# A state-space and attention trunk in one kernel: loads, low parts and stages of the state space parameters reordered

## The chip, the core and the metric

The kernel runs on one core of a Trainium2 chip: TensorE (PE; its weight loads are PEld), VectorE (DVE), ScalarE (ACT), GpSimd (POOL) and SyncE (SP, which only issues DMAs here). The metric is the device time in microseconds of one execution; lower is better. Each engine works its instructions off in program order; DMAs are issued from the queues of SP, ACT and POOL.

## What is computed

Two layers over x of 512 tokens by 2048 features, float32. Layer 0 mixes with a diagonal complex state space (S5), layer 1 with sparse attention over shared keys and values; each ends in a layer norm of the residual. The change touches the start of layer 0 only:

```python
def s5_mixer(x, w_in, lam_re, lam_im, log_dt, b_re, b_im, c_re, c_im, d_skip, w_glu, b_glu, w_out):
    u, z = jnp.split(x @ w_in, 2, axis=-1)          # 2048 -> 1024 + 1024
    dt = jnp.exp(log_dt)[:, None]                   # 64 groups
    mag = jnp.exp(lr * dt)
    ar, ai = mag * jnp.cos(li * dt), mag * jnp.sin(li * dt)     # 64 groups x 64 states
    ...                                             # b scaled by a function of ar, ai, lr, li
    h = scan(a, b u)                                # over the 512 tokens
    y = real(c h) + d_skip * u
    g = gelu(y)
    y = g * sigmoid(g @ w_glu + b_glu)
    return (y * silu(z)) @ w_out
```

## The kernel before

**Products in three parts.** TensorE multiplies in a reduced float32 form. Each operand is split into a high part (a cast on ScalarE) and a low part (value minus high part), and `mm3` issues three matmuls: high by high (L235), high by low (L236), low by high (L237). `Weights` streams weights in units of 128 x 1024: a load on SP's queue into one of 3 buffers, the cast on ScalarE (L78), the low part on VectorE (L85). From unit 11 (`DMA_FROM`) up to the gate weights the low part is made otherwise: ScalarE writes minus the high part (L81), and a DMA from GpSimd's queue adds the weights to it (L82). There are 3 buffers of split weights.

**The loop of layer 0** (`layer0_in`). x arrives in 16 slabs of 128 x 512 over 7 buffers. For each slab k: the load of slab k + 3, the cast (L788), the low part (L789: on VectorE for k in `XL_DVE`, on GpSimd for k = 2 to 9), and, on every second k, the split of the weight unit after the current one; then four `mm3`, one for each of the output tiles u0 to u3 that accumulate over all slabs. Units 0 to 8 serve this loop. Then come twelve tiles (`L0_TILES`: u4, z0, u5, z1, ...) of 16 `mm3` each, two units a tile: units 9 and 10 for u4, 11 and 12 for z0, 13 and 14 for u5. Unit j is split two `mm3` into the unit two before it.

**Work between the products.** `Background` holds four lanes of generators. After each `mm3` a tick adds 3 to a counter and advances one lane that is due (two lanes in the tiles), the one due longest first; a generator's yielded number is the gap until it is due again. So the counter fixes where an instruction stands in each engine's queue: 12 a slab, 192 for the loop, 48 a tile, 768 for all tiles. Nothing moves an instruction at run time.

**Lane 0 is the state space chain** (`S5.chain`). First the parameters (`params`), steps with a gap of `PACE`: the loads; three steps of exponential of the step size; four of sine and cosine of the angle, the last of which sets up the rotations on lane 2; three of exponential of the magnitude; then products, three doublings of powers and two small steps. All of it is VectorE work on 128x64 values. Then the letters of `START`, one every 3 counts: t is a step of the tables of group 0 (11 steps: six of VectorE work, two of TensorE products, a subtraction, a store, and the loads and transposes), p one of the tables of group 1, r one of the rotation of group 0, b waits for the end of the loop, a dot is an empty step. Then, for each of 8 groups of channels, the 18 tokens of `CYCLE` (54 counts): a is the scan of this group, t and p tables of the next two, r the next rotation.

**Lane 2** runs `turns` on GpSimd: 16 steps (`TPACE` 8) of repeated angle doublings (L465 to L479), products that fill two tables RB and RA (L484 to L489) and sign changes (L500, L502). A rotation (r) on VectorE reads these tables and waits for them in the program order.

**The queue of GpSimd before:** the zero fill of a DRAM buffer's padding (L342, L343), four loads of the two halves of lambda, the load of the step size broadcast over 128 rows (L369), then low parts of x, raw loads for tables (L350, L352), rotation steps and the DMAs of L82, in the order of the counter.

Of the kernel before, what the change touches and what calls it, by code (L numbers as in the profile page):

```python
# [11 lines left out]
F32 = mybir.dt.float32  # L12
# [3 lines left out]
OP = mybir.AluOpType  # L16
# [21 lines left out]
class Weights:  # L38
# [4 lines left out]
    def __init__(self, nc, pool, units):  # L43
        self.nc, self.pool, self.units = nc, pool, units
        self.extra, self.side, self.whole = {}, {}, set()
        self.pool_units = set()
        self.by_dma = set()
        self.raw, self.hl = {}, {}
        self.nd = self.ns = 0
# [261 lines left out]
def paced(gen, gap):  # L311
    for _ in gen:
        yield gap


PAD = 16 * (L - 1)


class S5:
# [6 lines left out]
    def __init__(self, c, sc, gT, bg):  # L326
        tc = c.tc
        self.bg, self.U = bg, {}
        self.u_d = c.dram.tile([8, GP, 16, L, NCH], F32, name="u_d")
        self.y_d = c.dram.tile([8, L, 16, GP, NCH], F32, name="ys_d")  # L330
        self.c, self.tc, self.nc, self.A, self.ident, self.gT = c, tc, tc.nc, c.A, c.ident, gT
        self.p1 = sc.enter_context(tc.tile_pool(name="s5p", reuse_waits="tile", bufs=1, side="right"))
        self.tb = sc.enter_context(tc.tile_pool(name="s5t", reuse_waits="tile", bufs=1, side="right"))
        self.ps = sc.enter_context(tc.tile_pool(name="s5ps", reuse_waits="tile", bufs=1, space=PSUM, side="right"))
        self.tab, self.raw, self.rot = {}, {}, {}
        self.summed = self.done = -1
        self.turned = False
        self.banks = False

        self.k_d = c.dram.tile([8, GP, 16, PAD + 128], F32, name="k_d")  # L340
        zero = self.tb.tile([64, PAD], F32, tag="ta", name="zero")
        self.nc.gpsimd.memset(zero, 0.0)  # L342
        self.nc.gpsimd.dma_start(self.k_d[:, :, :, :PAD].rearrange("t g c n -> (t g) c n"),  # L343
                                 zero.unsqueeze(1).to_broadcast([64, 16, PAD]))

    def load(self, ct):
        if ct >= 8 or ct in self.raw:
# [7 lines left out]
    def params(self):  # L355
        nc, A, p1 = self.nc, self.A, self.p1
        V, S, P, SP = nc.vector, nc.scalar, nc.gpsimd, nc.sync
        scratch = self.tb.tile([128, 18, G], F32, tag="W1", name="scratch", bufs=2)
        pw = self.tb.tile([128, 17 * G], F32, tag="tb", name="pw")
        slot = iter(range(18))  # L360

        def new(nm):
            return scratch[:, next(slot)]

        lr, li, ld = new("lr"), new("li"), new("ld")
        for h in range(2):
            P.dma_start(lr[64 * h:64 * h + 64], A["lam_re"])
            P.dma_start(li[64 * h:64 * h + 64], A["lam_im"])
        P.dma_start(ld, A["log_dt"].partition_broadcast(128))  # L369
        sg = p1.tile([128, 1], F32, name="sg")  # L370
        V.memset(sg[0:64], 1.0)
        V.memset(sg[64:128], -1.0)
        self.sg = sg
        dt, x, mag, th = new("dt"), new("x"), new("mag"), new("th")
        a, b, c, d = new("ta"), new("tb"), new("tc"), new("td")
        e = new("te")
        ni = new("ni").bitcast(I32)
        yield
        yield from exp_f32(V, ld, a, b, c, ni, dt)
        V.tensor_tensor(x, lr, dt, OP.mult)  # L380
        V.tensor_tensor(th, li, dt, OP.mult)
        sn, cs = new("sn"), new("cs")
        yield from sincos_f32(V, th, a, b, c, d, e, sn, cs)
        self.load(0)
        self.bg.add(2, self.turns(cs, sn, e, ld, dt, new("tf"), th, new("tg"), new("th2")))
        yield from exp_f32(V, x, a, b, c, ni, mag)
        yield
        X = pw[:, 512:].rearrange("p (g n) -> p g n", n=9)
        Y = p1.tile([128, G, 9], F32, name="Y")
        Xs = p1.tile([128, G, 9], F32, name="Xs")  # L390
        V.memset(X[:, :, 0:1], 1.0)
        V.memset(Y[:, :, 0:1], 0.0)
        ar, ai = X[:, :, 1], Y[:, :, 1]
        V.tensor_tensor(ar, mag, cs, OP.mult)
        V.tensor_tensor(ai, mag, sn, OP.mult)
        yield
        V.tensor_tensor(a, lr, lr, OP.mult)
        V.tensor_tensor(b, li, li, OP.mult)
        V.tensor_tensor(a, a, b, OP.add)
        inv = x  # L400
        V.reciprocal(inv, a)
        am1 = d
        V.tensor_scalar(am1, ar, -1.0, None, OP.add)
        cr = p1.tile([128, G], F32, name="cr")
        sci = p1.tile([128, G], F32, name="sci")
        V.tensor_tensor(a, am1, lr, OP.mult)
        V.tensor_tensor(b, ai, li, OP.mult)
        V.tensor_tensor(a, a, b, OP.add)
        V.tensor_tensor(cr, a, inv, OP.mult)
        V.tensor_tensor(a, ai, lr, OP.mult)  # L410
        V.tensor_tensor(b, am1, li, OP.mult)
        V.tensor_tensor(a, a, b, OP.subtract)
        V.tensor_tensor(a, a, inv, OP.mult)
        V.tensor_scalar(sci, a, sg, -1.0, OP.mult, OP.mult)
        self.cr, self.sci = cr, sci
        yield

        for lo, n in ((1, 1), (1, 2), (1, 4)):
            m = lo + n - 1
            shp = [128, G, n]  # L420
            xa, ya = X[:, :, lo:lo + n], Y[:, :, lo:lo + n]
            xm, ym = X[:, :, m:m + 1], Y[:, :, m:m + 1]
            if n > 1:
                xm, ym = xm.to_broadcast(shp), ym.to_broadcast(shp)
            t1 = pw[:, 0:256].rearrange("p (g n) -> p g n", n=4)[:, :, :n]
            t2 = pw[:, 256:512].rearrange("p (g n) -> p g n", n=4)[:, :, :n]
            dst = slice(m + 1, m + 1 + n)
            V.tensor_tensor(t1, xa, xm, OP.mult)
            V.tensor_tensor(t2, ya, ym, OP.mult)
            V.tensor_tensor(X[:, :, dst], t1, t2, OP.subtract)  # L430
            V.tensor_tensor(t1, xa, ym, OP.mult)
            V.tensor_tensor(t2, ya, xm, OP.mult)
            V.tensor_tensor(Y[:, :, dst], t1, t2, OP.add)
            yield
        V.tensor_scalar(Xs, X, sg, None, OP.mult)
        self.Y, self.Xs = Y, Xs
        yield

        m8 = p1.tile([128, G], F32, name="m8")
        V.tensor_tensor(m8, mag, mag, OP.mult)  # L440
        V.tensor_tensor(m8, m8, m8, OP.mult)
        V.tensor_tensor(m8, m8, m8, OP.mult)
        self.m8 = m8
        yield
# [236 lines left out]
    def chain(self):  # L681

        yield from paced(self.params(), PACE)
        t, p, r = self.tables(0), self.tables(1), self.rotation(0)
        for what in START:
            if what == "r":
# [20 lines left out]

XL_DVE = (0, 1, 10, 11, 12, 13, 14, 15)  # L710

TPACE = 8
PACE = 9

DMA_FROM = 11
EARLY = 2
# [2 lines left out]
SLOT = 3  # L719


START = 'ttttttb....ttttt.rprppp'
CYCLE = 'a a t a t a tt t rt ar a t a p a p ap p'

L0_TILES = [('u', 4), ('z', 0), ('u', 5), ('z', 1), ('u', 6), ('z', 2), ('z', 3), ('u', 7), ('z', 4), ('z', 5), ('z', 6), ('z', 7)]
# [2 lines left out]
def layer0_in(c, sc, sz_d):  # L728

    tc, nc, A, W, index, mm3, split = c.tc, c.nc, c.A, c.W, c.index, c.mm3, c.split  # L730
    V, S, P, PE, SP = nc.vector, nc.scalar, nc.gpsimd, nc.tensor, nc.sync
    xh = c.xp.tile([128, KD, T], F32R, tag="xh", name="xh")
    xl = c.xp.tile([128, KD, T], F32R, tag="xl", name="xl")
# [6 lines left out]
    bg = Background(4)  # L740
# [33 lines left out]
            SP.dma_start(xr[k], A["xT"][k])  # L774

    bg.add(0, s5.chain())
    pss = [pj.tile([128, T], F32, tag="ps", name="ps") for _ in range(2)]
    pss += [s5.ps.tile([128, T], F32, tag="tp", name="ps", bufs=2) for _ in range(2)]
    load_x(0)
# [3 lines left out]
    for u, ks in enumerate([(0,), (1,)] + [(k, k + 1) for k in range(2, KD, 2)]):  # L783
        h, l = W.get(u, 0, 1)
        for k in ks:
            load_x(k + 3)
            x = xr.pop(k)
            S.copy(xh[:, k], x)  # L788
            (V if k in XL_DVE else P).tensor_tensor(xl[:, k], x, xh[:, k].bitcast(F32), OP.subtract)  # L789
            if k == ks[-1]:  # L790
                W.ahead(u + 1)
            for n in range(4):
                lo = 512 * (k - ks[0]) + 128 * n
                ns = slice(lo, lo + 128)
                mm3(pss[n], h[:, ns], l[:, ns], xh[:, k], xl[:, k], k == 0, k == KD - 1)
                bg.tick()
# [9 lines left out]
    for what in L0_TILES:  # L806
# [4 lines left out]
        for u in range(2):  # L811
            h, l = W.get(index[what] + u, 1)
# [7 lines left out]
        n = what[1]  # L820
# [15 lines left out]
    for k in range(KE):  # L836
# [4 lines left out]
        for n in range(2):  # L841
            h, l = hls[n]
# [24 lines left out]
    for n in range(KE):  # L867
# [3 lines left out]
        else:  # L871
            h, l = W.get(index["w_glu", n])
# [4 lines left out]
        z = zs.pop(n)  # L877
# [766 lines left out]
```

## Time and profile before

| | |
|---|---|
| median of 3 runs (lowest, highest) | 1816.9 us (1815.18, 1820.62) |
| profiled execution | 1814.74 us, its span 1813.0 us |
| granted TensorE clock, mean over the span | 0.986 |
| busy, share of the span | PE 97%, PEld 80%, DVE 55%, ACT 33%, POOL 10% |
| HBM traffic | 188.42 MB read, 19.86 MB written, 115 GB/s |

The span runs from the first to the last instruction; the execution's time lies 1.7 us above it. Busy shares are means over stages that differ: the loop of layer 0 fills some 70 us, its tiles reach to 294 us, layer 1 takes the rest. A wait in brackets names the instruction whose end released the waiting one, as far as the semaphores show it.

### The profile page before, as it was taken

To read this page: it belongs to the slowest core of one execution; us is meant where nothing else is said; L and a number is where in the kernel's file an instruction comes from. 1 tells how busy PE (TensorE), PEld (TensorE's weight loads), DVE (VectorE), ACT (ScalarE), POOL (GpSimd) and SP (SyncE) were. 2 spreads that over 40 slices of the span, in tenths; PEclk is the share of its full clock that TensorE was granted. 3 is DMA by queue.
4 is the path that set the end of the run, shared out by engine and by line. 5 is a ranking of instruction groups with operands and counts; after the bars stand their busy time and mean duration, and the time that the engine had idled before them with its cause. 6 is when DMAs were issued, how large, how long until landed. Compare 5 with 4: busy or idle time off the path is not lost.

```text
span 1813.0 us, 21852 instructions
## 1 busy us (share of the span) xinstructions
PE 1753.1 (97%) x8455; PEld 1455.5 (80%) x8455; DVE 1005.7 (55%) x1807; ACT 605.3 (33%) x1018; POOL 187.7 (10%) x241
## 2 busy tenths in 40 slices
PE   6889999998999999999999999999999999999997
PEld 5668877886888888888888888888888888888886
DVE  7778863549333366553555553555543555665346
ACT  3344443323333333332333332333332333333120
POOL 5921100006100000000000000000000000010000
PEclk8999999999999999999999999999999999999999
DMA  5468774543333322222222222222222322236343
GB/s 202 147 151 213 199 178 127 197 151 135 128 102 119 105 82 87 76 87 82 87 70 87 87 76 93 87 77 81 88 87 82 99 76 82 76 115 233 127 140 104
DMA packets 89751, 209.70 MB, mean 116 GB/s; under 512 B 25264, under 2 KB 34720, under 8 KB 88624
## 3 DMA queue, kind: packets, MB, share of 16 engines
q1 hardware_dynamic: 81008, 181.31, 30.4%
q0 software_dynamic: 6336, 22.81, 5.3%
q10 hardware_dynamic: 2304, 4.20, 0.6%
q8 instruction: 66, 1.08, 0.2%
q14 instruction: 37, 0.30, 0.1%
HBM read 188.42 MB, written 19.86 MB: 115 GB/s over the span
## 4 chain that ended last, share of the span: by engine, by line
PE 81%; DVE 3%; ACT 1%; issue 0%; DVEq 0%; ACTq 0%
PE ps L235 23%; PE ps L237 23%; PE ps L236 23%; PE tp L1448 2%; PE s L237 1%; PE s L235 1%; PE s L236 1%; PE o L236 1%; PE o L237 1%; PE o L235 1%; DVE v L959 1%; PE cps L1213 1%; PE tp L1413 0%; PE tp L999 0%; PE o L1422 0%
## 5 line engine op out<-in xcount | busy, mean ns | idle before, releaser
L235 PE MATMUL ps<-x1h,hl 128*128 128x512 f32 (+1 forms) x1440 | 564.8, 392 | 1.6 <-ACT hl L78 1.6
L237 PE MATMUL ps<-x1h,hl 128*128 128x512 f32 (+1 forms) x1440 | 557.8, 387 | 0.5 <-DVE hl L85 0.5
L236 PE MATMUL ps<-x1l,hl 128*128 128x512 f32 (+1 forms) x1440 | 556.8, 387 | 0.0
L85 DVE TENSOR_TENSOR hl<-wr,hl 128x1024 fp32r<-128x1024 f32 (+1 forms) x247 | 300.6, 1221 | 321.0 <-ACT hl L78 317.4
L78 ACT CAST hl<-wr 128x1024 fp32r<-128x1024 f32 (+1 forms) x273 | 284.4, 1045 | 219.3 <-PE ps L237 185.5
L237 PEld LDWEIGHTS ps<-x1h,hl 128*128 128x128 f32 x1440 | 271.6, 189 | 57.1 <-DVE hl L85 1.0
L235 PEld LDWEIGHTS ps<-x1h,hl 128*128 128x128 f32 x1440 | 272.0, 189 | 48.2 <-ACT hl L78 1.8
L236 PEld LDWEIGHTS ps<-x1l,hl 128*128 128x128 f32 x1440 | 272.0, 189 | 46.2
L1385 ACT ACTIVATE p<-s,m 128x384 f32<-128x384 f32 (+3 forms) x128 | 67.6, 528 | 358.3 <-DVE m L1384 355.8
L1321 POOL TENSOR_TENSOR y<-y,z 128x512 f32<-128x512 f32 x32 | 41.5, 1296 | 999.8 <-DVE z L1320 863.0
L241 DVE TENSOR_TENSOR pl<-tp,ph 128x512 fp32r<-128x512 f32 (+3 forms) x128 | 61.9, 488 | 109.3 <-ACT ph L240 109.0
L236 PE MATMUL ps<-xl,hl 128*128 128x512 f32 x256 | 104.8, 409 | 11.9 <-DVE xl L789 6.9
L235 PE MATMUL ps<-xh,hl 128*128 128x512 f32 x256 | 110.3, 431 | 6.1 <-ACT xh L788 6.1
L237 PE MATMUL ps<-xh,hl 128*128 128x512 f32 x256 | 104.6, 409 | 6.2 <-DMA hl<-w_in_b 6.2
L240 ACT CAST ph<-tp 128x512 fp32r<-128x512 f32 (+3 forms) x128 | 54.1, 426 | 150.6 <-PE tp L1448 150.3
L235 PE MATMUL ps<-hl,y1h 128*128 128x512 f32 x256 | 99.7, 389 | 0.0
L236 PE MATMUL ps<-hl,y1h 128*128 128x512 f32 x256 | 99.6, 389 | 0.0
L237 PE MATMUL ps<-hl,y1l 128*128 128x512 f32 x256 | 99.6, 389 | 0.0
L236 PEld LDWEIGHTS ps<-xl,hl 128*128 128x128 f32 x256 | 50.8, 198 | 23.1 <-DVE xl L789 8.8
L1384 DVE TENSOR_REDUCE m<-s 128x1 f32<-128x384 f32 (+3 forms) x128 | 62.9, 491 | 4.4
L237 PEld LDWEIGHTS ps<-xh,hl 128*128 128x128 f32 x256 | 50.5, 197 | 18.4 <-DMA hl<-w_in_b 7.1
L1307 DVE SCALAR_TENSOR_TENSOR z<-z,ps 128x512 f32<-128x512 f32 x48 | 33.0, 688 | 57.5 <-ACT z L1306 57.4
(351 smaller groups left out, 2328.8 us busy)
## 6 DMA issues: line engine op xcount, KB each, us to landing
wr<-b_w_in SPq DMA_DIRECT2D x128, 512.0 KB, 3.2
wr<-kv_w SPq DMA_DIRECT2D x48, 512.0 KB, 3.2
wr<-b_w_out SPq DMA_DIRECT2D x32, 512.0 KB, 3.3
wr<-w_in_b SPq DMA_DIRECT2D x24, 512.0 KB, 3.7
hl<-w_in_b POOLq DMA_DIRECT2D x22, 512.0 KB, 6.4
wr<-w_out SPq DMA_DIRECT2D x16, 512.0 KB, 3.6
xr<-xT SPq DMA_DIRECT2D x16, 256.0 KB, 3.8
Tz<-k_d SPq DMA_DIRECT2D x64, 64.0 KB, 2.4
```

Of the source, the lines that this page charges most:

```text
L78: self.nc.scalar.copy(h[:, :n], r[:, :n])
L85: eng.tensor_tensor(l[:, :n], r[:, :n], h[:, :n].bitcast(F32), OP.subtract)
L235: PE.matmul(o, sh, mh, start=start, stop=False)
L236: PE.matmul(o, sh, ml, start=False, stop=False)
L237: PE.matmul(o, sl, mh, start=False, stop=stop)
L240: self.nc.scalar.copy(h, src)
L241: self.nc.vector.tensor_tensor(l, src, h.bitcast(F32), OP.subtract)
L1307: self.nc.vector.scalar_tensor_tensor(z, z, 1.0, ps, OP.add, OP.mult)
L1321: P.tensor_tensor(y[0], y[0], z, OP.add)
L1384: self.nc.vector.tensor_reduce(m[:, b - 1, i:i + 1], s, AX.X, OP.max, negate=True)
L1385: self.nc.scalar.activation(self.p[h, b][i], s, AF.Exp, bias=m[:, b - 1, i:i + 1], accum_out=self.sums[h, b][:, i:i + 1])
L1448: PE.transpose(tp[:, 128 * (i - j):128 * (i - j) + 128], p[i][:, at:at + 128], ident)
```

## The change

Four things. The step size is loaded first, ahead of lambda, and the zero fill comes behind these loads; the chain is advanced once before the loop instead of at the loop's first tick. All 16 low parts of x are made by VectorE. `PACE` goes from 9 to 12. `START` puts group 0's tables and three steps of group 1's tables ahead of the two rotation steps.

```diff
@@ -338,10 +338,6 @@
         self.banks = False
 
         self.k_d = c.dram.tile([8, GP, 16, PAD + 128], F32, name="k_d")
-        zero = self.tb.tile([64, PAD], F32, tag="ta", name="zero")
-        self.nc.gpsimd.memset(zero, 0.0)
-        self.nc.gpsimd.dma_start(self.k_d[:, :, :, :PAD].rearrange("t g c n -> (t g) c n"),
-                                 zero.unsqueeze(1).to_broadcast([64, 16, PAD]))
 
     def load(self, ct):
         if ct >= 8 or ct in self.raw:
@@ -363,10 +359,14 @@
             return scratch[:, next(slot)]
 
         lr, li, ld = new("lr"), new("li"), new("ld")
-        for h in range(2):
-            P.dma_start(lr[64 * h:64 * h + 64], A["lam_re"])
-            P.dma_start(li[64 * h:64 * h + 64], A["lam_im"])
         P.dma_start(ld, A["log_dt"].partition_broadcast(128))
+        for z, nm in ((lr, "lam_re"), (li, "lam_im")):
+            for h in range(2):
+                P.dma_start(z[64 * h:64 * h + 64], A[nm])
+        zero = self.tb.tile([64, PAD], F32, tag="ta", name="zero")
+        P.memset(zero, 0.0)
+        P.dma_start(self.k_d[:, :, :, :PAD].rearrange("t g c n -> (t g) c n"),
+                    zero.unsqueeze(1).to_broadcast([64, 16, PAD]))
         sg = p1.tile([128, 1], F32, name="sg")
         V.memset(sg[0:64], 1.0)
         V.memset(sg[64:128], -1.0)
@@ -707,10 +707,8 @@
 
 
 
-XL_DVE = (0, 1, 10, 11, 12, 13, 14, 15)
-
 TPACE = 8
-PACE = 9
+PACE = 12
 
 DMA_FROM = 11
 EARLY = 2
@@ -719,7 +717,7 @@
 SLOT = 3
 
 
-START = 'ttttttb....ttttt.rprppp'
+START = 'tttttt.b.tttttppp.rr.p'
 CYCLE = 'a a t a t a tt t rt ar a t a p a p ap p'
 
 L0_TILES = [('u', 4), ('z', 0), ('u', 5), ('z', 1), ('u', 6), ('z', 2), ('z', 3), ('u', 7), ('z', 4), ('z', 5), ('z', 6), ('z', 7)]
@@ -774,6 +772,7 @@
             SP.dma_start(xr[k], A["xT"][k])
 
     bg.add(0, s5.chain())
+    bg.advance(0)
     pss = [pj.tile([128, T], F32, tag="ps", name="ps") for _ in range(2)]
     pss += [s5.ps.tile([128, T], F32, tag="tp", name="ps", bufs=2) for _ in range(2)]
     load_x(0)
@@ -786,7 +785,7 @@
             load_x(k + 3)
             x = xr.pop(k)
             S.copy(xh[:, k], x)
-            (V if k in XL_DVE else P).tensor_tensor(xl[:, k], x, xh[:, k].bitcast(F32), OP.subtract)
+            V.tensor_tensor(xl[:, k], x, xh[:, k].bitcast(F32), OP.subtract)
             if k == ks[-1]:
                 W.ahead(u + 1)
             for n in range(4):
```

## Rows read from the trace of the kernel before

**Rows 1.** Stage table: busy us (instructions) of PE, PEld, DVE, ACT, POOL; clock; DMA.
```profile
45.00:50.00 5.00, 5.00 (x17) 3.96 (x16) 4.76 (x13) 1.15 (x3) 4.67 (x12) 0.68 0.25 89
...
150.00:200.00 50.00, 49.89 (x296) 41.91 (x295) 43.60 (x73) 21.99 (x32) 6.58 (x9) 1.00 0.83 206
```

**Rows 2.** Waits of TensorE, 0 to 520 us: waiter <- releaser: total us, times, longest.
```profile
PE ps L236 <- DVE xl L789: 6.9, 3, 4.4
...
PE ps L237 <- DMA hl<-w_in_b: 6.2, 2, 3.4
...
PE ps L236 <- POOL xl L789: 5.0, 2, 3.7
```

**Rows 3.** Timeline of TensorE: start, length, instruction, [idle before <- releaser].
```profile
16.11 0.80 PE L236 MATMUL ps<-xl,hl 128*128 128x512 f32 x1 [4.42 <-DVE xl L789]
...
67.94 0.50 PE L236 MATMUL ps<-xl,hl 128*128 128x512 f32 x1 [0.84 <-DVE xl L789]
...
70.33 0.39 PE L237 MATMUL ps<-xh,hl 128*128 128x512 f32 x1
...
88.77 0.50 PE L237 MATMUL ps<-xh,hl 128*128 128x512 f32 x1 [3.39 <-DMA hl<-w_in_b]
...
100.78 0.50 PE L237 MATMUL ps<-xh,hl 128*128 128x512 f32 x1 [2.86 <-DMA hl<-w_in_b]
...
111.76 0.43 PE L671 MATMUL yps<-e,W 128*128 128x64 f32 x2 [2.92 <-DVE e L637]
```

**Rows 4.** Timeline of VectorE, 12 to 89 us.
```profile
12.35 1.12 DVE L253 TENSOR_SCALAR scratch<-scratch 128x64 f32<-128x64 f32 x1 [4.26 <-DMA scratch<-log_dt]
...
15.37 0.69 DVE L789 TENSOR_TENSOR xl<-xr,xh 128x512 fp32r<-128x512 f32 x1
...
22.24 1.33 DVE L380 TENSOR_TENSOR scratch<-scratch 128x64 f32<-128x64 f32 x1
...
33.20 0.23 DVE L307 SCALAR_TENSOR_TENSOR scratch<-scratch 128x64 f32<-128x64 f32 x1
...
56.30 0.63 DVE L428 TENSOR_TENSOR pw<-pw 128x256 f32<-128x256 f32 x1
...
71.72 1.33 DVE L572 TENSOR_TENSOR ta<-Xs,B1s 128x1024 f32<-128x1024 f32 x1
...
88.78 1.28 DVE L518 TENSOR_TENSOR CS<-RA,RB 128x256 f32<-128x256 f32 x1 [7.96 <-POOL RB L487]
```

**Rows 5.** Timeline of GpSimd: three DMAs that its queue issues.
```profile
4.84 0.63 POOL L369 DMA_DIRECT2D scratch<-log_dt  x1
...
83.19 0.93 POOL L82 DMA_DIRECT2D hl<-w_in_b  x1
...
95.44 0.91 POOL L82 DMA_DIRECT2D hl<-w_in_b  x1
```

**Rows 6.** DMA issues, 0 to 20 us: count, KB each, us from issue to landing.
```profile
scratch<-log_dt POOLq DMA_DIRECT2D x1, 32.0 KB, 7.5
```

**Rows 7.** Timeline of ScalarE.
```profile
10.49 1.05 ACT L78 CAST hl<-wr 128x1024 fp32r<-128x1024 f32 x1 [1.71 <-DMA wr<-w_in_a]
...
74.02 1.06 ACT L81 ACTIVATE hl<-hl 128x1024 fp32r<-128x1024 f32 x1
...
118.24 0.60 ACT L746 ACTIVATE z<-ps 128x512 f32<-128x512 f32 x1
```

**Rows 8.** Groups by line and shape, GpSimd, 33 to 96 us: busy us, mean ns | idle.
```profile
L789 POOL TENSOR_TENSOR xl<-xr,xh 128x512 fp32r<-128x512 f32 x3 | 4.8, 1602 | 0.0
...
L486 POOL TENSOR_TENSOR RB<-RB 128x64 f32<-128x64 f32 x1 | 4.6, 4647 | 0.0
...
L486 POOL TENSOR_TENSOR RA<-RA 128x64 f32<-128x64 f32 x1 | 0.3, 313 | 0.0
```

**Rows 9.** Timeline of TensorE: work of the scan between the large matmuls.
```profile
92.74 1.00 PE L641 MATMUL s<-U,Bst 128*128 128x64 f32 x8
...
238.94 1.92 PE L580 MATMUL kps<-W,B 128*16 128x128 f32 x16
```

## Prediction

> **What bounds the kernel now.** I read the stage table first. From 150 to 200 us TensorE is busy 49.89 of 50 us at granted clock 1.00, while VectorE needs 43.60 of the 50 [rows 1]: a change of order wins nothing there, and VectorE has little room. The edits touch the first 120 us. The waits of TensorE name three causes there [rows 2]: low parts of x made by VectorE (6.9 us, 3 times), low parts of x made by GpSimd (5.0 us, twice) and low parts of weights that a DMA from GpSimd's queue adds up (6.2 us, twice). TensorE's timeline places them [rows 3]: 4.42 us before 16.11 (the second slab of x), 3.39 before 88.77 and 2.86 before 100.78 (units 11 and 12, the two halves of tile z0), 2.92 before 111.76 (the first scan's output). A long wait costs twice. In the stage behind the GpSimd wait of 3.7 us, 45 to 50 us, 17 matmuls started at clock 0.68 [rows 1]; at 0.23 us each, as from 67.94 to 70.33 [rows 3], 22 would have fitted: 1.2 us lost in that stage alone. I charge 1.5 to 2 us for each wait near 3 us or more.
>
> Behind each of these waits stands a queue that is worked off in order. VectorE's first parameter step waits 4.26 us for the step size, until 12.35, and the second low part of x is queued behind it, at 15.37 [rows 4]. The step size is the last of six loads on GpSimd's queue, issued at 4.84 [rows 5], and it took 7.5 us to land [rows 6]. The DMAs for units 11 and 12 issue at 83.19 and 95.44 [rows 5], behind rotation arithmetic on GpSimd, although ScalarE had unit 11 ready at 74.02 + 1.06 [rows 7]. VectorE itself stands 7.96 us before 88.78 [rows 4] for the same arithmetic, with the next group's tables queued behind.
>
> **The change, part by part.**
>
> *Step size first, zero fill last.* The issue moves from 4.84 to about 1.4, as 3.4 us of issuing (the zero fill, four lambda loads) go behind it. With the old 7.5 us it lands at 8.9, otherwise earlier; VectorE reaches the step near 8.0, so it waits 0 to 0.9 us. Either end is free for TensorE: the low part behind it is then made by 10.8, and TensorE stood for it from 16.11 - 4.42 = 11.7. The 4.42 us go, with 2 us of lower clock. The zero fill is read back tens of microseconds later, by the Toeplitz loads on the sync queue; behind it on GpSimd's queue comes nothing before the first raw load: nothing. Advancing the chain once ahead of the loop puts two memsets of a flag column where VectorE has no work yet: nothing.
>
> *Low parts of x on VectorE.* VectorE gets eight more slabs at 0.69 us [rows 4], 0.63 when queued: +5.0 us. It also loses clashes: while GpSimd split slabs, a 128x64 parameter instruction took 1.12 us at 12.35 and 1.33 at 22.24, where the one at 33.20 took 0.23 [rows 4]. I count six of those before 25 us, about 1 us each, so VectorE's sum hardly changes. TensorE's 5.0 us for GpSimd's low parts go, with 2 us of lower clock. The Trainium skill (SBUF — State Buffer, "Who interferes with whom") says that a VectorE instruction with two SBUF inputs and a GpSimd one that reads SBUF lock each other out for a whole instruction. By that rule, with which the 1.33 us agrees, the two slabs that newly fall beside the rotations would hold GpSimd up by 1.4 us and take as much from the gain.
>
> *Stages further apart.* Worked out from the scheduling counter (3 per group of three matmuls, 192 for the loop): the old parameter steps stand at 12, 21, 30 ... and the first table step at 174; the new ones at 12, 24, 36 ..., and, since the rotation lane wins three ties, the first table step at 240. Three parameter steps and five table steps leave the loop: 21 instructions, from the one at 56.30 to the one at 71.72 [rows 4] without the splits between, 12.8 us. With 5.0 added VectorE has nearly 8 us less to do inside the loop, so its other two late low parts (6.9 - 4.4 = 2.5 us [rows 2]) should go. One new wait: the long exponential polynomial is now queued ahead of the low part of k = 2. Its weights are cast at 10.49 + 1.05 [rows 7], split by 12.8; polynomial to 14.8 and low part to 15.4, where TensorE wants it at 14.2: 1.2 us.
>
> **Term A, the loop.** Its last matmul starts at 70.33 [rows 3] and ends near 70.5. Off come 4.4 + 5.0 + 2.5 and twice 2 for the clock, 15.9; on goes 1.2: it now ends near 55.8. A second way, from VectorE: some 36 us of instructions at their undisturbed durations stand between 12.8 and the last low part, so 49; if the rotations slow the last 20 of them by a fifth, 53, and TensorE ends 3 us later. Both agree.
>
> *Tables ahead of rotations, and GpSimd's chain.* The rotations may start once the cosine is done, at 33.4 [rows 4]. VectorE's queue from the low part at 15.37 + 0.69 to there took 17.4 us, 1.2 of it the split; the new one has five more slabs (+3.2) and lacks 3.6 us of the clashes: 15.8, from 12.8 on, so 28.6, 4.8 us earlier. The three slabs between the rotation steps leave, another 4.8 us [rows 8]. The chain ended as the DMA at 95.44 issued [rows 5]; now 85.8, if VectorE holds it up as much as before. No row shows the new overlap. One 128x64 instruction took 0.31 us by itself and 4.65 between VectorE's table multiplies [rows 8]. At the short durations the whole chain is some 39 us and done by 68; with its last 18 us held up by 10 more it ends at 96. I take 86: the same table work still falls on the same chain, two steps later in it.
>
> *What is queued behind it.* Unit 11's DMA stands one rotation step earlier in the chain, so it issues when ScalarE is ready: 75.1 - 70.5 = 4.6 us behind the loop's end, 60.4. It lands 5.5 us later (83.19 to 88.77, 95.44 to 100.78), at 65.9; z0 starts 48 matmuls behind the loop, at 66.7. No wait. Unit 12 comes behind two more rotation steps: 2.7 us of waiting (0.5 to 5). Unit 13, the first half of tile u5, now comes behind the whole chain and behind the next group's raw loads (1.2 us of issuing): 85.8 + 1.2 + 5.5 = 92.5, where TensorE could be there at 83: a new wait of up to 9 us. That is what is late next. The next group's tables wait for those raw loads too, to about 90; with the rotation behind them the first scan's output should be 2 us late, where it was 2.92.
>
> **Term B, at the start of u5.** Before, z0 ended as its tanh began, 118.2 [rows 7]; now 92.5, 25.7 earlier. Owed are pieces of group 0's scan and group 1's tables that the old order had done by then: 1.9 us of table products, twice 0.8 for the scan's input [rows 9], and some 2.4 (an estimate from such small matmuls) for transposes and most of the scan's output: 5.9. Off also 1.5 for the clock and 2 for the scan: 25.7 - 9.4 = 16.3 us. Behind that the new order is the old one 54 counts, one whole round of the scan cycle, later, so the steady stage stays. The last group's output lands at count 774, and the gate loop wants it at 810: 36 counts, 8 us, to spare. The profiled execution took 1814.7 us (span 1813.0): 1798.4. The median of the runs lies 2.2 higher: **1800**.
>
> **Rivals.**
> 1. *TensorE bounds.* With less beside it the chain ends before 75, and at most one low part is late. u5 starts at 55.8 + 21.8 + 2.8 = 80.4; 118.2 - 80.4 - 5.9 - 4 for remaining waits = 28: **1789**. For it: 39 us of short durations. Against: VectorE is still full beside it.
> 2. *VectorE bounds the loop.* Eight more slabs and the rotations stretch its last 20 us by 60% instead of a fifth: the loop ends at 64, the chain 8 us later, and the gain is 8: **1809**. For it: VectorE was busy 4.76 of 5 us in such a stage [rows 1]. Against: nearly 8 us leave the loop.
> 3. *The change doesn't do what it says.* What is won ahead of u5 is lost behind it: VectorE, with 6.4 of 50 us free [rows 1], holds TensorE up in the steady stage or in the later tail. Gain under 5: **1816**. Against: the orders match from one round on.
> 4. *Slower, by GpSimd's chain.* Its last 21 instructions meet table multiplies, and each waits one out, 1.3 us: 60 + 18.6 + 27 = 106. Unit 13 lands at 112.5, and the gain turns into a loss of 4: **1821**. It decides from a chain end of 102 on. Against: VectorE has some 9 us of such multiplies to put in the way, not 27.
>
> **How the numbers follow.** Forecast 0.62 (1792 to 1808 by itself), rivals 0.15, 0.11, 0.07 and 0.05. What a measurement of this kernel can tell from no change is about 0.3%, 5.5 us: faster 0.88, same 0.07, slower 0.05. The range 1787 to 1811 takes in the forecast and nearly all of rivals 1 and 2.
>
> **What would show it.** Right: no wait for the step size; the loop done at 54 to 58, with one wait for a low part near 15; rotations done at 82 to 90, and one wait of TensorE for a weight's low part ahead of u5; behind u5 only the 6 us owed. Wrong: a loop that ends after 61, a chain that ends after 96, or waits of TensorE past 130 us that the old kernel did not have.

## The result, and the profile after

| | before | after |
|---|---|---|
| median (lowest, highest) | 1816.4 us (1815.18, 1820.62) | 1803.7 us (1799.54, 1807.85) |
| profiled execution, its span | 1814.74, 1813.0 us | 1800.29, 1798.4 us |
| mean granted clock | 0.986 | 0.991 |

The ratio is 0.993, its 95% interval 0.990 to 0.995: faster by 9 to 18 us. The six times of the changed kernel stand in two groups, 1799.5 to 1800.3 us at a mean granted clock of 0.991 to 0.992 and 1807.1 to 1807.9 at 0.985 to 0.986; the profiled one is of the lower, the median lies between them, and no run settles what parts them.

The stage table shows where the time went. Its columns are those of [rows 1]: time, busy us (instructions) of PE, PEld, DVE, ACT and POOL, granted clock, DMA share, GB/s. First the kernel before:

```profile
0.00:50.00 50.00, 34.38 (x117) 26.54 (x118) 37.45 (x100) 16.48 (x23) 29.22 (x59) 0.86 0.56 190
50.00:100.00 50.00, 42.07 (x191) 32.55 (x189) 35.02 (x59) 14.81 (x23) 45.75 (x61) 0.97 0.49 138
100.00:150.00 50.00, 45.37 (x253) 37.88 (x254) 40.69 (x67) 24.48 (x35) 7.52 (x10) 0.93 0.72 183
```

The same stages after the change, and the steady one that [rows 1] shows of before:

```profile
0.00:50.00 50.00, 41.99 (x166) 33.45 (x167) 39.01 (x112) 19.55 (x27) 25.66 (x61) 0.97 0.63 216
50.00:100.00 50.00, 38.64 (x155) 29.12 (x154) 34.07 (x57) 19.20 (x27) 41.91 (x54) 0.88 0.60 154
100.00:150.00 50.00, 49.38 (x291) 41.99 (x291) 37.77 (x63) 21.45 (x31) 6.49 (x9) 0.98 0.72 184
150.00:200.00 50.00, 49.95 (x296) 41.98 (x295) 42.93 (x71) 21.72 (x32) 6.50 (x9) 1.00 0.88 217
```

Read the count of matmuls. After 50 us the new kernel is 49 ahead (166 against 117), after 100 us only 13, after 150 us 51. The loop is won, the stretch from 50 to 100 us gives nearly all of it back, and by 150 us a lead of 51, some 12 us at 0.23 each [rows 3], stands. (Matmuls of several sizes are counted alike, so this is rough.) The steady stage is what it was, 49.95 against 49.89 us.

TensorE's timeline after, its waits from the loop to u5 (start, length, instruction, [idle before <- releaser]):

```profile
16.48 0.79 PE L236 MATMUL ps<-xl,hl 128*128 128x512 f32 x1 [2.35 <-DVE xl L788]
...
70.24 0.50 PE L237 MATMUL ps<-xh,hl 128*128 128x512 f32 x1 [2.72 <-DMA hl<-w_in_b]
...
81.90 0.79 PE L237 MATMUL ps<-xh,hl 128*128 128x512 f32 x1 [4.29 <-DMA hl<-w_in_b]
...
98.05 0.57 PE L237 MATMUL ps<-xh,hl 128*128 128x512 f32 x1 [4.35 <-DMA hl<-w_in_b]
```

The waits of [rows 2] for low parts of x are down from 11.9 us to this one of 2.35 and one of 0.23; those for DMAed low parts of weights have grown from 6.2 us in two waits to 11.4 in three: units 11, 12 and now 13. GpSimd's timeline after shows their DMAs (L82) in its queue, where [rows 5] has those of before:

```profile
62.63 0.96 POOL L82 DMA_DIRECT2D hl<-w_in_b  x1
...
76.45 0.88 POOL L82 DMA_DIRECT2D hl<-w_in_b  x1
...
86.88 1.49 POOL L502 TENSOR_SCALAR nsb<-RB 128x512 f32<-128x512 f32 x1
88.31 0.62 POOL L346 DMA_DIRECT2D raw<-bc  x1
88.93 0.53 POOL L348 DMA_DIRECT2D dk<-d  x1
89.44 0.96 POOL L82 DMA_DIRECT2D hl<-w_in_b  x1
```

Unit 13's DMA is the last of these: behind the whole rotation arithmetic, which ends with the instruction at 86.88, and behind the raw loads of group 1.

### The profile page after: what moved, and what is told of

Its sections match the earlier page's. It is cut to its first block, busy times and chain, and to the rows that moved or that the text cites. A ratio compares the mean times of both kernels' runs of the same rounds, so it can differ in the third digit from the quotient of the medians.

```text
span 1798.4 us, 21845 instructions
## 1 busy us (share of the span) xinstructions
PE 1744.9 (97%) x8455; PEld 1448.5 (81%) x8455; DVE 1002.6 (56%) x1815; ACT 604.8 (34%) x1018; POOL 177.3 (10%) x233
## 4 chain that ended last, share of the span: by engine, by line
PE 81%; DVE 3%; ACT 1%; issue 0%; DVEq 0%; ACTq 0%
PE ps L235 23%; PE ps L237 23%; PE ps L236 23%; PE tp L1447 2%; PE s L237 1%; PE s L235 1%; PE s L236 1%; PE o L236 1%; PE o L237 1%; DVE v L958 1%; PE o L235 1%; PE cps L1212 1%; PE tp L1412 0%; PE o L1421 0%; DVE x1l L1002 0%
## 5 line engine op out<-in xcount | busy, mean ns | idle before, releaser
L237 PE MATMUL ps<-xh,hl 128*128 128x512 f32 x256 | 104.0, 406 | 11.4 <-DMA hl<-w_in_b 11.4
L237 PEld LDWEIGHTS ps<-xh,hl 128*128 128x128 f32 x256 | 50.1, 196 | 23.9 <-DMA hl<-w_in_b 12.6
L235 PEld LDWEIGHTS ps<-xh,hl 128*128 128x128 f32 x256 | 50.3, 197 | 16.1 <-ACT xh L787 5.6
```

Of the source, the lines that this page charges most:

```text
L235: PE.matmul(o, sh, mh, start=start, stop=False)
L237: PE.matmul(o, sl, mh, start=False, stop=stop)
```

## The experiments

The theory on record was the prediction's: the loop's waits are worth what its sum says, and the end of GpSimd's chain sets what is left. Rivals: one part alone carries the gain, or the chain's end costs nothing.

**One part at a time, on the kernel before.** *Step size first, zero fill last, one advance ahead of the loop:*

```diff
-        for h in range(2):
-            P.dma_start(lr[64 * h:64 * h + 64], A["lam_re"])
-            P.dma_start(li[64 * h:64 * h + 64], A["lam_im"])
         P.dma_start(ld, A["log_dt"].partition_broadcast(128))
+        for z, nm in ((lr, "lam_re"), (li, "lam_im")):
...
+    bg.advance(0)
```

> The kernel before with one part alone: the step size loaded first, the zero fill last, the chain advanced once ahead of the loop. Theory of the queues: the wait of 4.42 us at the second slab goes, and its 2 us of lower clock, so the loop ends some 6 us earlier; but GpSimd's rotations start only about 3 us earlier and end near 92 instead of 95.4, so the waits for units 12 and 13 grow and the whole gains about 3 us (ratio 0.998). Rival, that the waits of TensorE simply add up: 6 to 7 us (0.996).

Measured 1816.4 us, ratio 0.9997 (0.9988 to 1.0006): nothing, where the theory had 3 us and the rival 6 to 7. TensorE's timeline of this kernel:

```profile
25.98 0.79 PE L237 MATMUL ps<-xh,hl 128*128 128x512 f32 x1 [5.25 <-DVE hl L85]
...
58.95 0.62 PE L236 MATMUL ps<-xl,hl 128*128 128x512 f32 x1 [4.36 <-DVE xl L790]
...
90.34 0.79 PE L237 MATMUL ps<-xh,hl 128*128 128x512 f32 x1 [4.19 <-DMA hl<-w_in_b]
```

The wait of 4.42 us of [rows 3] is gone, and 5.25 us stand a little later for what VectorE, still as full, makes next. The last copy of a loop tile starts at 72.08 us, in before at 71.30.

*All low parts of x on VectorE:*

```diff
-            (V if k in XL_DVE else P).tensor_tensor(xl[:, k], x, xh[:, k].bitcast(F32), OP.subtract)
+            V.tensor_tensor(xl[:, k], x, xh[:, k].bitcast(F32), OP.subtract)
```

> The kernel before with one part alone: all 16 low parts of x on VectorE. Theory of the queues: GpSimd's chain loses 4.8 us of slabs and ends near 91; VectorE's clashes of about 5 us go and its eight more slabs of 5 us come; the gain is about 5 us (0.997). Rival, that the waits of TensorE add up: 5.0 for GpSimd's slabs and 2 of clock, 7 us (0.996). Rival, that VectorE bounds the loop: 0 or a loss, since the parameter steps still stand 9 apart and the low parts at k = 10 to 15 stay late.

Measured 1812.0, ratio 0.9976 (0.9966 to 0.9986): 4.3 us, close to the theory's 5. GpSimd's timeline:

```profile
89.14 1.49 POOL L502 TENSOR_SCALAR nsb<-RB 128x512 f32<-128x512 f32 x1
90.58 0.92 POOL L82 DMA_DIRECT2D hl<-w_in_b  x1
```

The chain ends 4.9 us earlier than in [rows 5] (90.58 for 95.44), and the gain is about that; the loop's last copy, at 68.16, is only 3.1 us earlier.

*Stages further apart, with the new order of letters:*

```diff
-PACE = 9
+PACE = 12
...
-START = 'ttttttb....ttttt.rprppp'
+START = 'tttttt.b.tttttppp.rr.p'
```

> The kernel before with one part alone: parameter steps 12 apart and the tables ahead of the rotations. Theory of the queues: the loop still waits for the step size and for GpSimd's slabs, so it ends only 2 to 3 us earlier; GpSimd's chain ends near 95 as before, but only unit 13 is behind its end, not unit 12, and VectorE does not stand for the rotations with tables queued behind; gain about 7 us (0.996). Rival, waits of the loop alone: 2.5 us (0.9985).

Measured 1807.5, ratio 0.9950 (0.9938 to 0.9962): 8.9 us, where 7 were expected. *`PACE` alone:*

```diff
-PACE = 9
+PACE = 12
```

> The kernel before with one number changed: parameter steps 12 counts apart instead of 9, the old order behind the loop, old loads, low parts shared with GpSimd. Theory: this number is the whole of e3 (9 us), since the first parameter step then stands at count 15, behind the second low part of x, which no longer waits for the step size, and VectorE has 12 us less to do inside the loop: about 1808. Rival, that the new order behind the loop carries half of e3: 1812 and above.

Measured 1803.6 (1802.19 to 1804.90), ratio 0.9931 (0.9916 to 0.9946): by the medians all that the four parts together give, from one number, and 4 us more than expected (by the profiled executions, 1802.19 and 1800.29, all but 1.9). Its VectorE timeline shows the first parameter step without a wait, though the step size is still loaded last:

```profile
8.94 0.69 DVE L789 TENSOR_TENSOR xl<-xr,xh 128x512 fp32r<-128x512 f32 x1 [0.54 <-ACT xh L788]
12.00 1.23 DVE L85 TENSOR_TENSOR hl<-wr,hl 128x1024 fp32r<-128x1024 f32 x1 [2.36 <-ACT hl L78]
13.14 1.30 DVE L253 TENSOR_SCALAR scratch<-scratch 128x64 f32<-128x64 f32 x1
```

Without the advance the loads stand at count 3 and the first step 12 later, behind the second low part of x (8.94) and a split (12.00). GpSimd's queue of the same kernel:

```profile
66.61 0.94 POOL L82 DMA_DIRECT2D hl<-w_in_b  x1
...
83.52 0.89 POOL L82 DMA_DIRECT2D hl<-w_in_b  x1
...
95.41 0.89 POOL L82 DMA_DIRECT2D hl<-w_in_b  x1
```

And TensorE, at the places where units 11, 12 and 13 land:

```profile
74.28 0.50 PE L237 MATMUL ps<-xh,hl 128*128 128x512 f32 x1 [2.18 <-DMA hl<-w_in_b]
...
89.02 0.80 PE L237 MATMUL ps<-xh,hl 128*128 128x512 f32 x1 [9.00 <-DMA hl<-w_in_b]
...
100.83 0.50 PE L237 MATMUL ps<-xh,hl 128*128 128x512 f32 x1 [0.82 <-DMA hl<-w_in_b]
```

Set these beside [rows 3] and [rows 5]. DMAs issue at 83.52 and 95.41, as in before at 83.19 and 95.44, and TensorE goes on at 89.02 and 100.83, as at 88.77 and 100.78. The chain ends when it did. But what lands at 89.0 is unit 12, where it was unit 11: `PACE` moves the rotation steps later in the counter, the units' DMAs stay where they are, so each DMA has one piece of the chain less ahead of it. No run moves this place alone, with the loop as it was; that the place carries the gain is read from these rows. Unit 12 is used 100.78 - 89.02 = 11.8 us earlier, and the execution is 12.6 us shorter (profiled 1802.19).

**The same from the other side, on the kernel after.** *Without the first part* (loads in the old order, no advance):

```diff
-        P.dma_start(ld, A["log_dt"].partition_broadcast(128))
...
-    bg.advance(0)
```

> The changed kernel with the first part undone: zero fill and lambda loaded ahead of the step size, no step of the chain ahead of the loop. Theory that GpSimd's chain paces the stretch up to the first scan: the chain starts some 3.5 us later and ends near 92, so 3 to 4 us are lost (about 1807). Rival, that this part does nothing, as it did alone (1816.43 against 1816.39): the time of the changed kernel, 1800 to 1804. Rival, that TensorE's wait of 4.42 us with its lower clock comes back in full: 6 to 7 us lost, 1810.

Measured 1805.2, ratio to before 0.9935 (0.9913 to 0.9957). That is within the spread of the changed kernel, so the times alone decide nothing. The trace goes with the theory: the DMAs for units 12 and 13 issue at 78.91 and 90.81, 2.5 and 1.4 us later, TensorE's wait for unit 12 is 8.49 us instead of 4.29, and the profiled execution, 1804.59, is 4.3 us longer. A part that is worth nothing alone may be worth something beside the others. *With the old order of letters:*

```diff
-START = 'tttttt.b.tttttppp.rr.p'
+START = 'ttttttb....ttttt.rprppp'
```

> The changed kernel with the old order of the steps behind the loop (rotation ahead of group 1's tables), parameter steps still 12 apart. Theory of GpSimd's chain: group 1's tables wait for their raw loads behind that chain in both orders, so the rotation runs while VectorE would stand anyway; the loss is 0 to 2 us. Rival, that tables ahead of rotations is what pays: 4 us or more lost, 1807 and above.

Measured 1799.7, ratio 0.9908 (0.9882 to 0.9934). The order brings nothing: twice, here and between the two spacing runs above, the kernel with the new letters is some 4 us behind the one with the old ones, with intervals that touch (3.0 and 5.7 us by the profiled executions). That it costs as much is likely, not shown.

**The chain's end.** *Six microseconds more at its end, without any effect on what is computed* (the last sign change is issued five times):

```diff
         P.tensor_scalar(self.nsb, RB[:, 1], -1.0, None, OP.mult)
+        for _ in range(4):
+            P.tensor_scalar(self.nsb, RB[:, 1], -1.0, None, OP.mult)
```

> The changed kernel with the last instruction of GpSimd's rotation chain issued five times instead of once (4 x 1.49 = 6 us more; the results are the same). Theory that the end of this chain paces the stretch up to the first scan, because unit 13's low part and group 1's raw loads stand behind it: 5 to 6 us longer than the changed kernel, about 1808. Rival, that VectorE's tables or the DMAs' own landing pace it: less than 2 us longer.

Measured 1807.5, profiled 1805.12 against 1800.29: 4 to 5 us. GpSimd and TensorE of this kernel:

```profile
87.31 6.21 POOL L504 TENSOR_SCALAR nsb<-RB 128x512 f32<-128x512 f32 x4
```

```profile
102.49 0.80 PE L237 MATMUL ps<-xh,hl 128*128 128x512 f32 x1 [10.06 <-DMA hl<-w_in_b]
```

Unit 13's wait goes from 4.35 to 10.06 us. *The chain shorter,* its three sign changes on VectorE:

```diff
-        for R in (RA, RB):
-            P.tensor_scalar(R[:, 1], R[:, 1], self.sg, None, OP.mult)
-        self.nsb = p1.tile([128, G, 8], F32, name="nsb")
-        P.tensor_scalar(self.nsb, RB[:, 1], -1.0, None, OP.mult)
...
+        if ct == 0:
+            for R in (self.RA, self.RB):
+                V.tensor_scalar(R[:, 1], R[:, 1], self.sg, None, OP.mult)
...
```

> The changed kernel with the last three instructions of GpSimd's rotation chain (0.92, 1.55 and 1.49 us, sign changes) made by VectorE at the first rotation step. Theory of the chain's end: unit 13's low part and group 1's raw loads issue 4 us earlier, and TensorE's wait of 4.35 us ahead of u5 goes: 3 to 4 us less than the changed kernel. Rival, that the wait for unit 12 (issued ahead of these three) or VectorE's 2 us for the sign changes take its place: within 1 us.

Measured 1797.3 (1796.65 to 1798.65), ratio 0.9897 (0.9881 to 0.9914): 6 us by the medians, 3 by the profiled executions (1797.40). Unit 13's DMA issues at 84.88 and is not waited for. Between the longer and the shorter chain this DMA moves from 94.60 to 84.88, by 9.7 us, and the medians by 10.2, with intervals that do not meet. So, up and down, the chain's end is paid for.

**What is queued behind it.** *Low parts of units 11 to 13 on VectorE:*

```diff
-DMA_FROM = 11
+DMA_FROM = 14
```

> The changed kernel with the low parts of units 11 to 13 made by VectorE as those of the units before them, not by a DMA from GpSimd's queue. Theory of the queues: what TensorE waits for ahead of u5 (2.72 + 4.29 + 4.35 us, and the lower clock behind) is the place of these DMAs behind the rotations; the waits go, 8 to 13 us less than the changed kernel, about 1792. Rival, that VectorE or the rotations bound there: three more subtractions of 1.2 us hold up GpSimd's chain, the wait moves to the scan's input or output, and the time stays within 3 us of the changed kernel's.

Measured 1802.8, ratio 0.9928 (0.9914 to 0.9942): no gain, where 8 to 13 us were expected; the rival had it right. All three waits for these DMAs are gone. GpSimd's and then VectorE's timeline:

```profile
70.30 6.06 POOL L485 TENSOR_TENSOR rtmp<-RB,scratch 128x512 f32<-128x512 f32 x1
...
87.96 0.63 POOL L346 DMA_DIRECT2D raw<-bc  x1
```

```profile
91.15 0.29 DVE L546 TENSOR_TENSOR ta<-raw,cr 128x128 f32<-128x128 f32 x1 [8.39 <-DMA raw<-bc]
```

The next in the same queue are the raw loads of group 1; VectorE now stands 8.39 us for them, and TensorE 4.09 us for a table product and 4.49 for the first scan's output. *The raw loads issued with those of group 0 as well:*

```diff
         self.load(0)
+        self.load(1)
...
-DMA_FROM = 11
+DMA_FROM = 14
```

> The changed kernel with units 11 to 13 split by VectorE (as in e4) and group 1's raw loads issued beside group 0's, ahead of the rotations on GpSimd. In e4 VectorE stood 8.39 us for those loads, until 91.15, and TensorE then 4.49 us for the scan's output. Theory of GpSimd's chain: that wait of VectorE goes, its tables run from 82 on, what is left to wait for is the end of the rotations at 86 to 88; 4 to 6 us less than e4, about 1797. Rival, that VectorE's own sum bounds: no more than 1 us less than e4.

Measured 1795.1, ratio 0.9879 (0.9859 to 0.9899): 7.7 us less by the medians, 3.5 by the profiled executions (1796.52), where 4 to 6 were expected. What is left is unit 14's DMA (3.71 us at 98.65) and 4.04 us of TensorE for a table product. *Unit 14 off the queue too, and six empty letters ahead of the tables:*

```diff
-DMA_FROM = 14
+DMA_FROM = 15
...
-START = 'tttttt.b.tttttppp.rr.p'
+START = 'tttttt.b.....tttttppp..rr..p'
```

> As f3, with unit 14 split by VectorE too and six empty steps more (18 counts) among the steps behind the loop, so that TensorE has 4 us more of large matmuls ahead of the first scan. Theory: every wait of TensorE between loop and scan loses about 4 us of what f3 leaves; 3 to 6 us less than f3, about 1793; the last group's output then lands 12 counts before it is wanted, and TensorE may stand for it 1 us in the gate loop. Rival, that the later chain costs at the gate loop what it wins at the first scan: the time of f3.

Measured 1786.8 (1786.43 to 1790.87), ratio 0.9838 (0.9818 to 0.9858): 17 us better than the changed kernel by the medians, 13 by the fastest execution of each. This last step changes two things, and no run parts unit 14's place from the six empty letters. TensorE's waits from 50 to 100 us, and then that stage in the table:

```profile
77.50 1.05 PE L581 MATMUL kps<-W,B 128*16 128x128 f32 x8 [1.35 <-DVE W L567]
85.87 1.38 PE L603 MATMUL qps<-ident,ta 128*128 128x128 f32 x8 [3.20 <-DVE ta L586]
```

```profile
50.00:100.00 50.00, 45.25 (x208) 36.03 (x207) 45.96 (x65) 17.29 (x25) 43.70 (x49) 0.97 0.48 138
```

208 matmuls where the changed kernel has 155, the clock at 0.97 for 0.88, though the chain ends later than there (L82 at 92.02) and the loop no sooner (last copy at 57.01, for 56.78). *Both, the shorter chain on top:* three operations more on VectorE, as above.

> f4_all_off_chain with the three sign changes of the rotations' tables on VectorE, as in g3_chain_shorter. Theory (the end of GpSimd's chain holds what is queued behind it, and in f4 no low part of the weights and no raw load is queued there any more): the chain's end comes 3 to 5 us earlier, but only the tables' own readers wait for it, so of the 5 us that the same edit gave in g3 at most 1 to 3 are left: 1784 to 1786 us against 1786.8, and no wait of TensorE between 60 and 105 us over 4 us. Rival (the chain's length is paid at every place, whatever is queued behind it): again 5 us, 1782 us. A second rival (VectorE is by now what bounds the loop, and three more operations there cost their own time, some 1 to 2 us): 1787 to 1789 us.

Measured 1786.0 (1784.66 to 1790.85), ratio 0.9841 (0.9823 to 0.9858). By the medians the edit that was worth 3 to 6 us is worth 0.8, less than these runs can tell from nothing, although GpSimd's last rotation instruction now ends at 85.0 where its chain ended at 92.0. The profiled executions lie 4.9 us apart (1790.87, the longest of its kernel, and 1785.93), but not by the stretch that the chain is in. ScalarE reads the last of the twelve tiles here, in the changed kernel, with the shorter chain, with everything off the queue, and with both:

```profile
280.40 0.60 ACT L744 ACTIVATE z<-ps 128x512 f32<-128x512 f32 x1 [2.75 <-PE ps L237]
...
275.71 0.60 ACT L745 ACTIVATE z<-ps 128x512 f32<-128x512 f32 x1 [2.76 <-PE ps L237]
...
265.71 0.60 ACT L745 ACTIVATE z<-ps 128x512 f32<-128x512 f32 x1 [0.40 <-ACT gy L677]
...
264.20 0.60 ACT L746 ACTIVATE z<-ps 128x512 f32<-128x512 f32 x1 [0.40 <-ACT gy L678]
```

Their loops' last copies start at 56.78, 56.31, 57.01 and 55.19, so from there to the last tile they take 223.6, 219.4, 208.7 and 209.0 us. The shorter chain saves 4.2 us there in the changed kernel, and nothing where TensorE needs nothing soon from behind it.

Side by side (us; where the last copy of a loop tile starts, where the chain has ended, the median):

| kernel | loop | chain | median |
|---|---|---|---|
| before | 71.30 | 95.44 | 1816.4 |
| step size first | 72.08 | 94.42 | 1816.4 |
| low parts on VectorE | 68.16 | 90.58 | 1812.0 |
| `PACE` 12 | 61.35 | 95.41, unit 12 ahead of its end | 1803.6 |
| after | 56.78 | 88.31, unit 12 ahead of its end | 1803.7 |
| units 11 to 14 and raw loads off the queue, six empty letters | 57.01 | 92.02, neither behind it | 1786.8 |

The time follows what TensorE needs from behind the chain, not when the loop ends: from the fourth to the fifth row the loop gains 4.6 us and the median nothing (the profiled execution 1.9). Nor is it the chain's end by itself, which gains 7.1 us there: unit 13, which then also stands behind the raw loads and is longer in landing, is used only 2.8 us earlier (98.05 for 100.83).

## Why the prediction was right, point by point

The forecast of 1798.4 us for the profiled execution met 1800.29, the median of 1800 met 1803.7, inside the range. Step by step:

*The loop's end: right.* Predicted 55.8. The last copy starts 71.30 - 56.78 = 14.5 us earlier, where 14.7 were forecast. The one wait near 15 us came too, 2.35 us where 1.2 had been worked out. VectorE's timeline has the step size without a wait, and the cosine (L307), which releases the rotations, close to the 28.6 that were predicted:

```profile
9.05 0.19 DVE L253 TENSOR_SCALAR scratch<-scratch 128x64 f32<-128x64 f32 x1
...
19.03 0.22 DVE L380 TENSOR_TENSOR scratch<-scratch 128x64 f32<-128x64 f32 x1
...
29.16 0.23 DVE L307 SCALAR_TENSOR_TENSOR scratch<-scratch 128x64 f32<-128x64 f32 x1
```

L253 and L380 took 1.12 and 1.33 us in [rows 4]: the clashes with GpSimd's splits are gone as worked out.

*The share of each part in that: wrong.* Term A gave the step size 4.4 + 2 us, GpSimd's slabs 5.0 + 2, the spacing 2.5. Alone they bring 0, 4.3 and 12.7 us of the execution's time. The step that failed is "The 4.42 us go, with 2 us of lower clock", as a term that can be added: with VectorE as full as before, the wait comes back behind the next split. And the spacing alone removes the same wait for the step size, so the parts overlap. The order of letters, the fourth part, brings nothing.

*GpSimd's chain: right, 2.6 us off.* Predicted end 85.8, measured 88.4. It started at 29.47 instead of 28.6, and ran 1.7 us longer than the rows without slabs gave. The Trainium skill's rule on VectorE and GpSimd (SBUF — State Buffer, "Who interferes with whom") had been worked out to 1.4 us for the two new slabs; the size agrees, though no run shows that it is by them.

*The waits for units 11 to 13: right in kind, off in size.* Unit 11 was to cost nothing and cost 2.72, unit 12 2.7 and cost 4.29, unit 13 was to land at 92.5 and came at 98.05. One term that failed is "It lands 5.5 us later", from two rows: from issue to TensorE's start it was 70.24 - 62.63 = 7.6, 81.90 - 76.45 = 5.5 and 98.05 - 89.44 = 8.6 us. The other is the issue. Unit 11's did not come "when ScalarE is ready" (59.75 + 1.06 = 60.81) but behind a piece of the chain, at 62.63 for 60.4; unit 13's came at 89.44 for 87.0, as the chain ended later. So 2.4 of unit 13's 5.5 us are the issue and 3.1 the landing. A third term hid part of this: "TensorE could be there at 83". It was there at 98.05 - 4.35 = 93.7, and so waited 4.35 us and not 9. It had lost the waits for units 11 and 12 on the way, and the clock behind them, granted at 0.66 from 70 to 75 us and at 0.50, the lower of its two levels (1.2 GHz), from 82 to 88. Of the signs that the prediction named, the one wait for a weight's low part ahead of u5 did not come: there were two, and a third at u5 itself.

*Term B: right, by errors against each other.* The lead at u5 was to be 25.7 us. The kernel before reached u5's first low part here:

```profile
119.33 0.40 PE L237 MATMUL ps<-xh,hl 128*128 128x512 f32 x1
```

So the lead there is 119.33 - 98.05 = 21.3. The work still owed is paid at the end of the tiles. ScalarE reads the last two of them here in before, and the last but one here in after (its last stands above):

```profile
283.38 0.60 ACT L746 ACTIVATE z<-ps 128x512 f32<-128x512 f32 x1 [3.32 <-PE ps L237]
...
294.26 0.60 ACT L746 ACTIVATE z<-ps 128x512 f32<-128x512 f32 x1 [4.38 <-PE ps L237]
```

```profile
262.87 0.60 ACT L744 ACTIVATE z<-ps 128x512 f32<-128x512 f32 x1 [4.34 <-PE ps L237]
```

At the last but one the lead is 283.38 - 262.87 = 20.5: of the 1.5 us charged for the clock and the 2 for the first scan's output only 0.8 are lost, as TensorE does not wait for that output. At the last it is 294.26 - 280.40 = 13.9, 6.6 less, where 5.9 had been charged. Behind the tiles TensorE waits 0.9 us longer for ScalarE's gate values (3.8 for 2.9), and yet the lead at the end is 1814.74 - 1800.29 = 14.45; what gives the rest back is not shown. That 16.3 us were forecast and 14.45 measured is therefore partly luck.

*Cause and place.* The prediction saw that unit 11's DMA stands one step earlier in the chain and unit 13's behind all of it, but it booked this as the removal of two waits, and the gain as the loop's. The `PACE` run shows it the other way round: the loop's 10 us are lost again in one wait of 9.00 us, and what stays is, as its rows show it, the one place by which the DMAs moved up the queue.

*The rivals.* TensorE never bound (rival 1, 1789): three waits stood in the way, and with their causes and unit 14's gone, and the tables six letters later, 1787 was reached. The loop did not stretch (rival 2). From u5 on no more was lost than the work owed (rival 3): the steady stage is equal. Rival 4's mechanism is real, but the chain ended at 88, far from the 102 from which it would have decided; the longer chain shows its slope, 4 to 5 us for 6.

What stays open: why a DMA of the same size comes in 5.5 or in 8.6 us, what a DMA's place in the queue is worth with the loop unchanged, and how the last 8 us, from 1795.1 to 1786.8, divide between unit 14's place and the empty letters.

## What to carry to other kernels

Where a late wait is released from an in-order queue, find what stands ahead of it there: a gain upstream is kept only as far as that instruction moves up the queue or the work ahead of it ends sooner. When one thing is taken out from behind such a chain, look at the next one behind it, which may cost as much: here the first removal paid nothing, and each of the next two some 8 us by the medians. And run each part of a change by itself: the sum was right here for a split that was not, and one part, worth nothing alone, seems to be worth some 4 us beside the others.

## What the runs showed of the hardware

One GpSimd instruction on 128x512 lasted 6.06 us (the row at 70.30, with units 11 to 13 split on VectorE) while VectorE went through five instructions with two SBUF inputs without a gap, four of the tables and one split:

```profile
70.41 1.34 DVE L561 TENSOR_TENSOR ta<-Xs,raw 128x1152 f32<-128x1152 f32 x1
71.68 1.34 DVE L563 TENSOR_TENSOR tb<-Y,raw 128x1152 f32<-128x1152 f32 x1
72.95 1.21 DVE L85 TENSOR_TENSOR hl<-wr,hl 128x1024 fp32r<-128x1024 f32 x1
74.08 1.34 DVE L566 TENSOR_TENSOR W<-ta,tb 128x1152 f32<-128x1152 f32 x1
75.46 1.99 DVE L572 TENSOR_TENSOR ta<-Xs,B1s 128x1024 f32<-128x1024 f32 x1
```

The same instruction took 1.34 us in the changed kernel, where VectorE stood idle. The Trainium skill (SBUF — State Buffer, "Who interferes with whom") has the later of two such instructions wait until the first is done; here the wait outlasted four of VectorE's, of 1.21 to 1.34 us each. And an accumulating DMA of 512 KB from GpSimd's queue let TensorE go on 5.5 to 8.6 us after its issue, in the three cases that TensorE waited for in the changed kernel.
